# A seven-product feed-forward: matrix sums of the weight blocks made earlier, on VectorE, and kept in device memory

## The chip, the cores and the metric

One core of one Trainium2 chip runs the whole program. The metric is the device time of one execution in microseconds (us). Engines: TensorE (PE; its weight loads are PEld), VectorE (DVE), ScalarE (ACT), GpSimd (POOL), SyncE (SP, which issues the DMAs here).

## The reference

Two layers over 512 tokens of width 1024, in float32. Each layer mixes tokens in three ways (a gated delta net, a sparse attention, a gated recurrence), projects the result back, and then runs a feed-forward block. Only this block matters here:

```python
def conv_geglu_ffn(h, w_up, conv_w, w_down):
    up = causal_depthwise_conv(h @ w_up, conv_w)
    gate, val = jnp.split(up, 2, axis=-1)
    return (jax.nn.gelu(gate, approximate=True) * val) @ w_down
...
    x = x + rmsnorm(conv_geglu_ffn(h, ffn_w_up[l], ffn_conv[l], ffn_w_down[l]), g_ffn_post[l])
```

`w_up` is 1024 x 5632, `w_down` is 2816 x 1024.

## The kernel before

Every float32 product is made of three matmuls on split operands: an operand is rounded to a high part by ACT (line 123, `split`), and the low part is the difference, a subtraction on DVE or on POOL (line 124). The names end in h or hi and l or lo.

**The up stage** (`ffn`, line 927 on) goes over 22 pairs of column tiles (j). For each of the 44 tiles, `project` loads one weight tile of 512 KB (`wraw`, two buffers), splits it (`whi`, `wlo`, two buffers each) and runs 24 matmuls of 512 columns into one of two accumulators `p_mm` (lines 181 to 183). `conv` then reads the accumulator, with one ACT pass (line 198) and two DVE passes (line 200), into `u`. DVE multiplies gate and value (line 944). After every odd j, two pairs are combined into the left operands of one block: `as` and `ad` (high and low), `ax`, and the plain sum tile `ak`. So there are 11 blocks, each with 256 rows of `w_down`.

**The down stage** (`down_seven`, line 961 on) computes the 2 x 2 block product with seven products in place of eight, so it needs sums and differences of the four 128 x 512 quarters of each weight block. The quarters arrive as two 512 KB tiles, x and y (both called `wx`). There are two sweeps over the 11 blocks:

- the first (`first_weights`) splits y, makes two sums on DVE (lines 1008, 1009), splits x, and splits `ak` on POOL (`kl`). Its products 2, 1, 6 and 5 take 24 matmuls of a block (line 983);
- the second (`second_weights`) loads x and y again, makes two differences on DVE (lines 1027, 1029) and one sum on POOL (line 1031), and splits the three results, two on DVE, one on POOL (`dl`, `ql`, `wm`). It takes 18 matmuls of a block.

The raw tiles use the six buffers of the up weights (`wraw`, `whi`, `wlo`) in turn, so three blocks are in flight. The split results use four wide tiles (`wm`, two blocks in flight) or small slots of the pool of 68 (`act`). The last blocks' products are held back (`keep`, `hold`) so that they cover the closing norms.

Each engine runs its instructions in a fixed order, which a scheduler sets when the program is built; the order of the calls in the code and the priorities (`first()`) steer it. SP issues all DMAs one after the other; an issue that waits holds those behind it.

Of the kernel before, what the change touches and what calls it, by code (L numbers as in the profile page):

```python
# [9 lines left out]
F32 = mybir.dt.float32  # L10
# [3 lines left out]
OP = mybir.AluOpType  # L14
# [4 lines left out]
T = 512  # L19
P = 128  # L20
NB = 4
D = 1024
KT = 8
NIN = 30
NFF = 22
# [14 lines left out]
def hybrid_encoder_kernel(ctx: ExitStack, tc: tile.TileContext, x, win, wout, wup, wdn, gall, gates,  # L40
                          dncw, ffcw, vecs, hglb, consts, out):
    nc = tc.nc
    V, S, G, PE, SP = nc.vector, nc.scalar, nc.gpsimd, nc.tensor, nc.sync
# [3 lines left out]
    ring = ctx.enter_context(tc.tile_pool(name="ring", bufs=2))  # L47
    ps = ctx.enter_context(tc.tile_pool(name="ps", bufs=2, space=PSUM))

    def first(n=1):  # L50
        return tc.high_priority(offset=n * FIRST)
# [70 lines left out]
    def split(src, hi, lo, eng=V):  # L122
        S.activation(hi, src, AF.Copy)  # L123
        eng.tensor_tensor(lo, src, hi.bitcast(F32), op=OP.subtract)  # L124
# [71 lines left out]
    def conv(dst, acc, w, taps):  # L196
        with first():
            S.activation(dst, acc, AF.Copy, scale=w[:, taps - 1:taps])  # L198
            for s in range(1, taps):
                V.scalar_tensor_tensor(dst[:, s:], acc[:, :T - s], w[:, taps - 1 - s:taps - s], dst[:, s:],  # L200
                                       op0=OP.mult, op1=OP.add)
# [709 lines left out]
    def slot(pool, name, dt=F32R):  # L911
        return pool.tile([P, T], dt, name=name, tag="act", bufs=ACT_SLOTS)
# [10 lines left out]
    def ffn(l, hid, pool, extra):  # L923
        cw = pool.tile([P, 2 * P], F32, name="fcw", tag="fcw", bufs=1)[:, :6 * NFF].rearrange("p (j s) -> p j s", s=3)
        SP.dma_start(cw, ffcw[l])
        half = lambda z, r: z.rearrange("p (i r c) -> p i r c", r=2, c=P)[:, :, r]
        part = lambda z, r: z[:, 2 * P * r:2 * P * r + 2 * P]
        side = lambda z, r: part(z, r).rearrange("p (i c) -> p i c", c=P)
        left, accs, last = [], [], None
        for j in range(NFF):  # L930
            up = pool.tile([P, 2 * T], F32, name="u", tag="u", bufs=2)
            uv = [up[:, :T], up[:, T:]]
            for i in range(2):
                if not accs:
                    n = 3 if j == 0 else 1
                    accs, last = project(hid, [wup[l, 2 * j + i + m] for m in range(n)], COLS2 if n > 1 else ((0, T),),
                                         extra=extra)
                conv(uv[i], accs.pop(0), cw[:, 2 * j + i], 3)
            gelu = S.activation(uv[0], uv[0], AF.Gelu_apprx_tanh)  # L939
            if j % 2 == 0:  # L940
                same, cross = slot(pool, "ak", F32), slot(pool, "ar", F32)
            for r in range(2):
                to = same if r == j % 2 else cross
                V.tensor_tensor(side(to, r), half(uv[0], r), half(uv[1], r), op=OP.mult)
            if j % 2 == 0:
                continue
            rows, both = [[slot(pool, n) for n in (f"{m}h", f"{m}l")] for m in ("as", "ad")]
            diff = slot(pool, "ax")
            V.tensor_tensor(uv[0], same, cross, op=OP.add)  # L949
            split(uv[0], *rows)  # L950
            V.tensor_tensor(part(uv[1], 0), part(cross, 1), part(same, 0), op=OP.subtract)
            V.tensor_tensor(part(uv[1], 1), part(same, 0), part(same, 1), op=OP.add)
            split(uv[1], *both)
            V.tensor_tensor(part(cross, 0), part(cross, 0), part(same, 1), op=OP.subtract)
            split(part(cross, 0), part(diff, 0), part(diff, 1))
            left.append((rows, both, (part(diff, 0), part(diff, 1)), same))
        explog(gelu)
        return left, last

    def down_seven(pool, left, src, gp, xs, finish, after):  # L960
        n = len(left)
        keep, hold = 4, 8
        loads = [0]
        M = {"2": [do("m2"), po_("m2")], "1": [dn("m1"), dn("m1")], "6": [ds("m6"), ds("m6")], "5": [mm("m5"), mm("m5")]}
        begun = set()

        def raw(j):
            k = loads[0]
            loads[0] += 1
            tags = ("wraw", "wraw") if k < 2 or k % 3 == 1 else ("whi", "wlo")  # L970
            xy = [ring.tile([P, D], F32, name="wx", tag=t, bufs=2) for t in tags]
            for i in (1, 0):
                SP.dma_start(xy[i], src[i, j])
            return xy

        def quarter(z, i):
            return z[:, i * T:(i + 1) * T]
# [12 lines left out]
        def wide():  # L990
            return [base.tile([P, 4, T], F32R, name="wm", tag="ht", bufs=4) for _ in range(2)]

        def first_weights(j):
            x, y = raw(j)
            if j == 0:
                ops = [[ring.tile([P, D], F32R, name=t, tag=t, bufs=2) for t in ("whi", "wlo")] for _ in range(2)]
                ya, za = ops
                yw = [[quarter(t, i) for t in ya] for i in range(2)]
                zw = [[quarter(t, i) for t in za] for i in range(2)]
            else:  # L1000
                w = wide()
                ya = [t[:, 0:2].rearrange("p i t -> p (i t)") for t in w]
                za = [t[:, 2:4].rearrange("p i t -> p (i t)") for t in w]
                yw = [[t[:, i] for t in w] for i in range(2)]
                zw = [[t[:, 2 + i] for t in w] for i in range(2)]
            with first():
                split(y, *ya)
                V.tensor_tensor(quarter(x, 0), quarter(x, 0), quarter(y, 1), op=OP.add)
                V.tensor_tensor(quarter(x, 1), quarter(y, 0), quarter(y, 1), op=OP.add)
                split(x, *za)  # L1010
            same = left[j][3]
            kh, kl = slot(pool, "kh"), slot(pool, "kl")
            split(same, kh, kl, G)
            left[j] = left[j][:3] + ((kh, kl),)
            return yw, zw

        def second_weights(j):
            x, y = raw(j)
            if 2 <= j < n - keep:
                w = wide()  # L1020
                dw = [[t[:, i] for t in w] for i in range(3)]
                if j >= n - hold:
                    dw[2] = [slot(pool, "qh"), slot(pool, "ql")]
            else:
                dw = [[slot(pool, "dh"), slot(pool, "dl")] for _ in range(3)]
            with first():
                V.tensor_tensor(quarter(y, 1), quarter(x, 1), quarter(y, 1), op=OP.subtract)  # L1027
                split(quarter(y, 1), *dw[1])
                V.tensor_tensor(quarter(x, 0), quarter(x, 0), quarter(y, 0), op=OP.subtract)
                split(quarter(x, 0), *dw[0])  # L1030
                G.tensor_tensor(quarter(x, 1), quarter(x, 1), quarter(y, 0), op=OP.add)  # L1031
                split(quarter(x, 1), *dw[2], G)
            return dw

        xv = []
# [16 lines left out]
        for i in range(2):  # L1052
            t = slot(pool, "yt", F32)
# [26 lines left out]
        for j in range(2, n):  # L1080
            dw = second_weights(j)
# [33 lines left out]
    hid = Hidden()  # L1115
    with tc.tile_pool(name="start", bufs=1, reuse_waits="tile") as pool:
        xs = load_x(pool, 1)
# [11 lines left out]
    for l in range(L):  # L1129
        hid = mix_phase(l, hid)  # L1130
        with tc.tile_pool(name="ffn", bufs=1, reuse_waits="tile") as pool:
            extra = lambda: [slot(pool, "fw") for _ in range(2)]
            left, last = ffn(l, hid, pool, extra)
            row = lambda k, i: lambda c: bass.AP(tensor=gall.tensor, offset=gall.offset + (k * 4 + i) * D + c.start,
                                                 ap=[[0, P], [1, T]])
            gp = lambda: Halves(pool, "gp", row(l, 3))
            xs = lambda b: Halves(pool, "xb", lambda c: xd[b][:, c])
            if l + 1 < L:
                gn = []
                hid2 = Hidden()  # L1140

                def finish(b, xb):
                    if not gn:
                        gn.append(Halves(pool, "gn", row(l + 1, 0)))
                    norm_block(pool, hid2, b, xb, gn[0], tag="u")
                    xd[b] = tc.dram_tile([P, D], F32, name="xd")
                    for q in range(2):
                        SP.dma_start(xd[b][:, q * T:(q + 1) * T], xb[:, q * T:(q + 1) * T])
            else:
                def finish(b, xb):  # L1150
                    for q in range(2):
                        SP.dma_start(out[b * P:(b + 1) * P, q * T:(q + 1) * T], xb[:, q * T:(q + 1) * T])
            down_seven(pool, left, wdn[l], gp, xs, finish, last)
        hid = hid2


# [78 lines left out]
```

## Time and profile before

| | us |
|---|---|
| median of 3 runs (lowest, highest) | 1446.74 (1445.73, 1454.11) |
| the profiled execution: its own time | 1458.69 |
| the profiled execution: span from first to last instruction | 1456.8 |

All stretches and durations come from the profiled execution, which is 11.95 us longer than the median; differences worked out in it are taken over to the median as they stand. In the trace, the up stages run from 386 to 609.6 us (layer 0) and from 1098 to 1321.1 us (layer 1), the down stages from 609.6 to 738.7 and from 1321.1 to 1449.4 us. Line L983 is `add`, the products of the down stage; L181 to L183 are those of the up stage. An engine's busy share says little by itself: what counts is which engine the others wait for in a stage.

### The profile page before, as it was taken

What the parts mean: (1) busy time and instruction counts of PE and PEld (TensorE: products, weight loads), DVE (VectorE), ACT (ScalarE), POOL (GpSimd) and SP (SyncE); (2) the same over time, 40 slices, a digit from 0 to 9 for tenths busy, and PEclk for the clock granted to TensorE, in tenths of its full rate; (3) what the DMA queues carried; (4) which work ended last, traced back from release to release, by engine and by line L of the source; (5) the groups of instructions that cost most, each with busy time, mean ns of one, the idle gap of its engine ahead of it and who ended that gap; (6) DMA issues with size and microseconds to landing.
All of it is one profiled execution on the core that took longest, in us unless ns stands there. A gap on an engine that the chain in (4) does not pass through costs nothing.

```text
span 1456.8 us, 20429 instructions
## 1 busy us (share of the span) xinstructions
PE 1370.6 (94%) x7560; PEld 1113.0 (76%) x7560; DVE 1110.1 (76%) x1967; ACT 736.2 (51%) x1395; POOL 223.8 (15%) x160
## 2 busy tenths in 40 slices
PE   6999989999999999989789999899999999999987
PEld 5787767868888888767578877678788888886765
DVE  4599974786767767799875999779666776768988
ACT  4355854555543444453453558565654443444533
POOL 2032210010000000054520322102000000003353
PEclk9999996999999999999999999999999999999998
DMA  4433320025233233386524233201342232235852
GB/s 161 121 94 109 102 57 19 15 73 188 89 101 101 88 102 101 115 293 194 180 100 126 88 109 102 59 17 52 123 147 89 100 100 94 95 102 184 280 193 94
DMA packets 59459, 166.04 MB, mean 114 GB/s; under 512 B 15264, under 2 KB 16224, under 8 KB 59360
## 3 DMA queue, kind: packets, MB, share of 16 engines
q1 hardware_dynamic: 59360, 164.73, 34.6%
q8 instruction: 60, 0.98, 0.3%
q14 instruction: 39, 0.32, 0.1%
HBM read 152.36 MB, written 8.95 MB: 111 GB/s over the span
## 4 chain that ended last, share of the span: by engine, by line
PE 64%; DVE 23%; ACT 5%; issue 4%; DMA 3%; POOL 0%; SPq 0%; DVEq 0%; POOLq 0%; ACTq 0%
PE p_mm L182 14%; PE p_mm L183 14%; PE p_mm L181 14%; PE p_m L983 5%; DVE sc L394 3%; DMA wx<-in_wdn_dram 3%; DVE wm L124 3%; DVE m L393 2%; PE p_dn L225 2%; PE p_dn L226 2%; PE p_dn L220 2%; DVE qkv L200 1%; DVE wx L1027 1%; DVE dl L124 1%; DVE wlo L124 1%
## 5 line engine op out<-in xcount | busy, mean ns | idle before, releaser
L181 PE MATMUL p_mm<-hhi,whi 128*128 128x512 f32 (+1 forms) x1232 | 474.4, 386 | 4.1 <-DVE qkv L200 3.9
L182 PE MATMUL p_mm<-hlo,whi 128*128 128x512 f32 (+1 forms) x1232 | 474.2, 385 | 1.6 <-DVE hlo L177 1.6
L183 PE MATMUL p_mm<-hhi,wlo 128*128 128x512 f32 (+1 forms) x1232 | 474.1, 385 | 0.0
L124 DVE TENSOR_TENSOR wlo<-wraw,whi 128x1024 fp32r<-128x1024 f32 x132 | 163.2, 1236 | 176.1 <-ACT whi L123 173.7
L123 ACT ACTIVATE whi<-wraw 128x1024 fp32r<-128x1024 f32 x156 | 165.1, 1058 | 240.9 <-PE p_mm L182 205.9
L181 PEld LDWEIGHTS p_mm<-hhi,whi 128*128 128x128 f32 x1232 | 234.4, 191 | 48.4 <-ACT qkv L198 4.4
L182 PEld LDWEIGHTS p_mm<-hlo,whi 128*128 128x128 f32 x1232 | 234.8, 191 | 44.6 <-DVE hlo L177 2.8
L183 PEld LDWEIGHTS p_mm<-hhi,wlo 128*128 128x128 f32 x1232 | 235.0, 191 | 42.5 <-issue 0.5
L124 POOL TENSOR_TENSOR kl<-ak,kh 128x512 fp32r<-128x512 f32 x22 | 40.4, 1853 | 651.7 <-ACT kh L123 644.9
L200 DVE SCALAR_TENSOR_TENSOR u<-p_mm,fcw,u 128x511 f32<-128x511 f32 (+1 forms) x172 | 128.2, 745 | 7.8 <-ACT u L198 5.5
L124 POOL TENSOR_TENSOR wlo<-wraw,whi 128x1024 fp32r<-128x1024 f32 x24 | 57.5, 2396 | 260.3 <-PE p_mm L183 93.8
L123 ACT ACTIVATE wm<-wx 128x1024 fp32r<-128x1024 f32 (+1 forms) x62 | 53.9, 900 | 63.9 <-PE p_m L983 27.0
L124 DVE TENSOR_TENSOR wm<-wx,wm 128x1024 fp32r<-128x1024 f32 (+1 forms) x60 | 78.0, 1327 | 9.2 <-ACT wm L123 8.9
L939 ACT ACTIVATE u<-u 128x512 f32<-128x512 f32 x44 | 27.9, 633 | 72.9 <-DVE u L200 72.9
L983 PE MATMUL p_m<-wm,ash 128*128 128x512 f32 x160 | 52.2, 399 | 6.9 <-DVE wm L124 5.2
L198 ACT ACTIVATE u<-p_mm,fcw 128x512 f32<-128x512 f32 x86 | 57.6, 670 | 0.0
L200 DVE SCALAR_TENSOR_TENSOR qkv<-p_mm,cw,qkv 128x511 f32<-128x511 f32 (+2 forms) x72 | 53.0, 739 | 5.1 <-ACT qkv L198 4.8
L123 ACT ACTIVATE ash<-u 128x512 fp32r<-128x512 f32 x22 | 14.0, 634 | 80.4 <-DVE u L949 80.4
L983 PE MATMUL p_m<-wm,adh 128*128 128x512 f32 x160 | 52.1, 402 | 2.2 <-DVE wm L124 1.6
L393 DVE MAX8 m<-sc 128x8 f32<-128x512 f32 (+2 forms) x96 | 52.8, 554 | 1.0
L394 DVE MATCH_REPLACE8 sc<-m,sc 128x512 f32<-128x512 f32 (+2 forms) x96 | 51.9, 541 | 0.0
L1031 POOL TENSOR_TENSOR wx<-wx 128x512 f32<-128x512 f32 x22 | 36.6, 1664 | 52.1 <-DVE wx L1027 52.1
(367 smaller groups left out, 2427.0 us busy)
## 6 DMA issues: line engine op xcount, KB each, us to landing
wraw<-in_wup_dram SPq DMA_DIRECT2D x88, 512.0 KB, 3.4
wx<-in_wdn_dram SPq DMA_DIRECT2D x88, 512.0 KB, 4.6
wraw<-in_win_dram SPq DMA_DIRECT2D x60, 512.0 KB, 3.5
wraw<-in_wout_dram SPq DMA_DIRECT2D x16, 512.0 KB, 3.5
xb<-in_x_dram SPq DMA_DIRECT2D x8, 512.0 KB, 6.3
E<-dr SPq DMA_DIRECT2D x8, 512.0 KB, 3.7
xd<-xb SPq DMA_DIRECT2D x8, 512.0 KB, 2.7
xb<-xd SPq DMA_DIRECT2D x16, 256.0 KB, 5.9
```

The source lines that it names most:

```text
L123: S.activation(hi, src, AF.Copy)
L124: eng.tensor_tensor(lo, src, hi.bitcast(F32), op=OP.subtract)
L181: PE.matmul(out_, ah, bh, start=start, stop=False)
L182: PE.matmul(out_, ah, bl, start=False, stop=False)
L183: return PE.matmul(out_, al, bh, start=False, stop=stop)
L198: S.activation(dst, acc, AF.Copy, scale=w[:, taps - 1:taps])
L200: V.scalar_tensor_tensor(dst[:, s:], acc[:, :T - s], w[:, taps - 1 - s:taps - s], dst[:, s:], op0=OP.mult, op1=OP.add)
L220: first = PE.matmul(acc[b], th[:, bs], piece(hi, i, T), start=k == 0, stop=False)
L393: V.max(m8, bias)
L394: V.match_replace(bias, m8, bias, REPL)
L983: p = PE.matmul(M[m][i], al(a[x]), w[y], start=first_, stop=False, skip_group_check=True)
L1031: G.tensor_tensor(quarter(x, 1), quarter(x, 1), quarter(y, 0), op=OP.add)
```

## The change

The five sums and differences of each block move from the two sweeps of the down stage to the up stage. A new function, `weight_sums`, is called at j = 1, 2, 4, 6, 7, 9, 11, 12, 14, 16 and 17. It loads the four quarters in four DMAs of 256 KB, makes the five results with five DVE operations of 128 x 512, and stores them in five DMAs of 256 KB to a scratch tensor in device memory (`wsz`, `wsx`, `wsq`). The sweeps load the results: y and z (512 KB each) in the first, x (512 KB) and q (256 KB) in the second, and only split them. All splits of the sweeps, `kl` and the third one of the second sweep too, are on DVE; POOL has no part in them. `hold` goes from 8 to 6. ACT's roundings and the number of matmuls stay.

```diff
@@ ffn
-        left, accs, last = [], [], None
+        left, accs, last, sums = [], [], None, []
         for j in range(NFF):
+            if len(sums) < NFF // 2 and j % 5 not in (0, 3):
+                sums.append(weight_sums(pool, wdn[l], len(sums)))
...
+    def weight_sums(pool, src, j):
+        x, y, z = [[slot(pool, f"w{m}", F32) for _ in range(2)] for m in "xyz"]
+        for i, t in ((0, x), (1, y)):
+            for q in range(2):
+                SP.dma_start(t[q], src[i, j, :, q * T:(q + 1) * T])
+        for out_, a, b, op in ((z[0], x[0], y[1], OP.add), (z[1], y[0], y[1], OP.add), (x[0], x[0], y[0], OP.subtract),
+                               (y[0], x[1], y[0], OP.add), (x[1], x[1], y[1], OP.subtract)):
+            V.tensor_tensor(out_, a, b, op=op)
+        dz, dx, dq = [tc.dram_tile([P, c], F32, name=f"ws{m}") for m, c in (("z", D), ("x", D), ("q", T))]
+        for d, t in ((dz, z), (dx, x), (dq, y[:1])):
+            for q, h in enumerate(t):
+                SP.dma_start(d[:, q * T:(q + 1) * T], h)
+        return dz, dx, dq
...
@@ down_seven
-        keep, hold = 4, 8
+        keep, hold = 4, 6
...
@@ first_weights
-            x, y = raw(j)
+            y, z = raw(src[1, j], sums[j][0])
...
             with first():
                 split(y, *ya)
-                V.tensor_tensor(quarter(x, 0), quarter(x, 0), quarter(y, 1), op=OP.add)
-                V.tensor_tensor(quarter(x, 1), quarter(y, 0), quarter(y, 1), op=OP.add)
-                split(x, *za)
+                split(z, *za)
             same = left[j][3]
             kh, kl = slot(pool, "kh"), slot(pool, "kl")
-            split(same, kh, kl, G)
+            split(same, kh, kl)
@@ second_weights
-            x, y = raw(j)
+            x, q = raw(sums[j][1], sums[j][2])
...
             with first():
-                V.tensor_tensor(quarter(y, 1), quarter(x, 1), quarter(y, 1), op=OP.subtract)
-                split(quarter(y, 1), *dw[1])
-                V.tensor_tensor(quarter(x, 0), quarter(x, 0), quarter(y, 0), op=OP.subtract)
+                split(quarter(x, 1), *dw[1])
                 split(quarter(x, 0), *dw[0])
-                G.tensor_tensor(quarter(x, 1), quarter(x, 1), quarter(y, 0), op=OP.add)
-                split(quarter(x, 1), *dw[2], G)
+                split(q, *dw[2])
```

Where the instructions go, first on DVE in the up stage of layer 0, around the pairs j = 6 and 7. `wlo` is the split of an up weight, L200 the convolution, `ar` and `ak` the gated products. Before:

```order
L124 TENSOR_TENSOR wlo<-wraw,whi 128x1024
L200 SCALAR_TENSOR_TENSOR u<-p_mm,fcw,u 128x511
L200 SCALAR_TENSOR_TENSOR u<-p_mm,fcw,u 128x510
L944 TENSOR_TENSOR ar<-u 128x256
L944 TENSOR_TENSOR ak<-u 128x256
L949 TENSOR_TENSOR u<-ak,ar 128x512
L951 TENSOR_TENSOR u<-ar,ak 128x256
L952 TENSOR_TENSOR u<-ak 128x256
L954 TENSOR_TENSOR ar<-ar,ak 128x256
L124 TENSOR_TENSOR asl<-u,ash 128x512
L200 SCALAR_TENSOR_TENSOR u<-p_mm,fcw,u 128x511
L124 TENSOR_TENSOR wlo<-wraw,whi 128x1024
```

And now (lines of the changed file; L969 are the new sums):

```order
L124 TENSOR_TENSOR wlo<-wraw,whi 128x1024
L200 SCALAR_TENSOR_TENSOR u<-p_mm,fcw,u 128x511
L200 SCALAR_TENSOR_TENSOR u<-p_mm,fcw,u 128x510
L946 TENSOR_TENSOR ar<-u 128x256
L946 TENSOR_TENSOR ak<-u 128x256
L951 TENSOR_TENSOR u<-ak,ar 128x512
L953 TENSOR_TENSOR u<-ar,ak 128x256
L969 TENSOR_TENSOR wz<-wx,wy 128x512
L969 TENSOR_TENSOR wz<-wy 128x512
L124 TENSOR_TENSOR wlo<-wraw,whi 128x1024
L200 SCALAR_TENSOR_TENSOR u<-p_mm,fcw,u 128x511
L969 TENSOR_TENSOR wx<-wx,wy 128x512
```

The sums stand ahead of the next `wlo` and between the two passes of a convolution; what they displace (`ar`, `asl`) comes later.

On SP, at the start of the up stage of layer 0, the 40 loads of up weights stood in one row; now each sum's loads and stores stand among them (- before, + now; `wraw` is an up weight, `wx` and `wy` the four quarters, `wsz`, `wsx`, `wsq` the stores):

```order
 L925 DMA fcw<-in_ffcw_dram 128x132
-L130 DMA wraw<-in_wup_dram 128x1024 x40
-L973 DMA wx<-in_wdn_dram 128x1024 x13
+L130 DMA wraw<-in_wup_dram 128x1024 x3
+L966 DMA wx<-in_wdn_dram 128x512 x2
+L966 DMA wy<-in_wdn_dram 128x512 x2
+L130 DMA wraw<-in_wup_dram 128x1024
+L973 DMA wsz<-wz 128x512 x2
+L973 DMA wsx<-wx 128x512
+L973 DMA wsq<-wy 128x512
```

An up weight's load now stands behind four loads or behind three or four stores that wait for DVE. The loads of a sum are issued one up weight ahead of the sums that use them.

On DVE at the start of the second sweep (`yu` combines finished products, `wm` are split results). Before:

```order
L1064 TENSOR_TENSOR yu<-p_m_5373,yt 128x512
L1027 TENSOR_TENSOR wx<-wx 128x512
L1029 TENSOR_TENSOR wx<-wx 128x512
L1027 TENSOR_TENSOR wx<-wx 128x512
L124 TENSOR_TENSOR wm<-wx,wm 128x512 x4
L1029 TENSOR_TENSOR wx<-wx 128x512
```

Now:

```order
L1077 TENSOR_TENSOR yu<-p_m_5626,yt 128x512
L124 TENSOR_TENSOR wm<-wx,wm 128x512 x5
L124 TENSOR_TENSOR ql<-wx,qh 128x512 x2
L124 TENSOR_TENSOR wm<-wx,wm 128x512 x5
L124 TENSOR_TENSOR dl<-wx,dh 128x512 x5
```

Only splits are left there; `ql`, and the `dl` that were POOL's, have joined them.

## Rows read from the trace of the kernel before

**Rows 1.** The page: busy time of each engine, its share of the span, instructions.
```profile
PE 1370.6 (94%) x7560; PEld 1113.0 (76%) x7560; DVE 1110.1 (76%) x1967; ACT 736.2 (51%) x1395; POOL 223.8 (15%) x160
```

**Rows 2.** Busy time by stage: up, down, up, down; the last three columns are clock, DMA, rate.
```profile
386.00:609.60 223.60, 223.60 (x990) 185.23 (x990) 156.36 (x239) 94.58 (x135) 0.00 (x0) 1.00 0.30 97
609.60:738.70 129.10, 114.37 (x471) 88.01 (x469) 116.67 (x126) 60.85 (x102) 56.02 (x34) 0.97 0.65 216
1098.00:1321.10 223.10, 223.10 (x986) 184.76 (x986) 155.91 (x238) 93.90 (x135) 0.00 (x0) 1.00 0.30 96
1321.10:1449.40 128.30, 115.22 (x463) 88.43 (x462) 113.80 (x122) 56.62 (x90) 55.49 (x33) 0.95 0.59 200
```

**Rows 3.** PE in order of time: a tile's first matmul, each down stage's first and last.
```profile
604.16 0.39 PE L181 MATMUL p_mm<-hhi,whi 128*128 128x512 f32 x1
...
609.60 0.39 PE L983 MATMUL p_m<-whi,ash 128*128 128x512 f32 x1
...
738.46 0.39 PE L983 MATMUL p_m<-dh,ax 128*128 128x512 f32 x1
...
1321.14 0.39 PE L983 MATMUL p_m<-whi,ash 128*128 128x512 f32 x1
...
1449.06 0.39 PE L983 MATMUL p_m<-dh,ax 128*128 128x512 f32 x1
```

**Rows 4.** PE's waits in the down stage of layer 0: total us, times, longest.
```profile
PE p_m L983 <- DVE wm L124: 6.7, 4, 2.8
PE p_m L983 <- ACT wm L123: 3.4, 4, 2.4
```

**Rows 5.** Groups of the down stage, layer 0: busy, mean ns; idle before, what ended it.
```profile
L124 DVE TENSOR_TENSOR wm<-wx,wm 128x1024 fp32r<-128x1024 f32 x20 | 28.6, 1447 | 2.1 <-ACT wm L123 2.1
L1027 DVE TENSOR_TENSOR wx<-wx 128x512 f32<-128x512 f32 x11 | 11.9, 1081 | 4.1 <-DMA wx<-in_wdn_dram 2.8 <-POOL wx L1031 1.3
L1031 POOL TENSOR_TENSOR wx<-wx 128x512 f32<-128x512 f32 x11 | 18.3, 1667 | 25.8 <-DVE wx L1027 25.8
L123 ACT ACTIVATE wm<-wx 128x1024 fp32r<-128x1024 f32 x20 | 20.7, 1055 | 21.7 <-DVE wx L1009 10.8 <-PE p_m L983 10.0 <-DMA wx<-in_wdn_dram 0.7
```

**Rows 6.** DVE, then POOL, in order of time in the second sweep.
```profile
709.17 1.78 DVE L1027 TENSOR_TENSOR wx<-wx 128x512 f32<-128x512 f32 x1
710.87 0.68 DVE L1029 TENSOR_TENSOR wx<-wx 128x512 f32<-128x512 f32 x1
...
708.84 1.56 POOL L124 TENSOR_TENSOR dl<-wx,dh 128x512 fp32r<-128x512 f32 x1 [0.74 <-ACT dh L123]
```

**Rows 7.** Stretches of 4 us, columns as in rows 2: full traffic, a slow clock, stores.
```profile
618.00:622.00 4.00, 3.68 (x15) 2.16 (x13) 3.28 (x5) 2.02 (x3) 0.00 (x0) 1.00 0.93 370
698.00:702.00 4.00, 2.89 (x7) 2.34 (x8) 3.88 (x4) 1.67 (x3) 2.06 (x2) 0.54 0.46 147
1438.00:1442.00 4.00, 4.00 (x19) 3.34 (x18) 3.21 (x6) 1.80 (x6) 0.00 (x0) 1.00 0.34 131
```

**Rows 8.** Groups on DVE in the up stage of layer 0.
```profile
L124 DVE TENSOR_TENSOR wlo<-wraw,whi 128x1024 fp32r<-128x1024 f32 x40 | 49.0, 1225 | 62.6 <-ACT whi L123 62.5
L949 DVE TENSOR_TENSOR u<-ak,ar 128x512 f32<-128x512 f32 x10 | 6.9, 692 | 0.3
```

**Rows 9.** One tile's period in the up stage: ACT, then DVE, in order of time.
```profile
598.70 1.06 ACT L123 ACTIVATE whi<-wraw 128x1024 fp32r<-128x1024 f32 x1 [0.76 <-PE p_mm L182]
...
599.79 1.23 DVE L124 TENSOR_TENSOR wlo<-wraw,whi 128x1024 fp32r<-128x1024 f32 x1 [1.64 <-ACT whi L123]
600.93 1.53 DVE L200 SCALAR_TENSOR_TENSOR u<-p_mm,fcw,u 128x511 f32<-128x511 f32 x2
```

**Rows 10.** DMA issues (KB, median us to landing); last, `wx`: minimum, median, maximum.
```profile
wraw<-in_wup_dram SPq DMA_DIRECT2D x88, 512.0 KB, 3.4
xb<-xd SPq DMA_DIRECT2D x16, 256.0 KB, 5.9
...
DMA to landing us min/median/max: 3.3/4.6/7.6
```

More of the change, by code (lines that the diff above doesn't have):

```diff
@@ L957, in ffn, with down_seven @@
         explog(gelu)
-        return left, last
-    def down_seven(pool, left, src, gp, xs, finish, after):
+        return left, last, sums
+    def weight_sums(pool, src, j):
[11 more added lines that the diff above has]
+        return dz, dx, dq
+    def down_seven(pool, left, sums, src, gp, xs, finish, after):
         n = len(left)
-        keep, hold = 4, 8
+        keep, hold = 4, 6
         loads = [0]
@@ L965, in down_seven, with raw @@
         begun = set()
-        def raw(j):
+        def raw(*from_):
             k = loads[0]
@@ L970, in raw @@
             tags = ("wraw", "wraw") if k < 2 or k % 3 == 1 else ("whi", "wlo")
[L971 to L974, printed above, removed]
+            got = []
+            for f, t in zip(from_, tags):
+                r = ring.tile([P, D], F32, name="wx", tag=t, bufs=2)[:, :f.shape[-1]]
+                SP.dma_start(r, f)
+                got.append(r)
+            return got
         def quarter(z, i):
@@ L1132, in hybrid_encoder_kernel @@
             extra = lambda: [slot(pool, "fw") for _ in range(2)]
-            left, last = ffn(l, hid, pool, extra)
+            left, last, sums = ffn(l, hid, pool, extra)
             row = lambda k, i: lambda c: bass.AP(tensor=gall.tensor, offset=gall.offset + (k * 4 + i) * D + c.start,
@@ L1152, in finish @@
                         SP.dma_start(out[b * P:(b + 1) * P, q * T:(q + 1) * T], xb[:, q * T:(q + 1) * T])
-            down_seven(pool, left, wdn[l], gp, xs, finish, last)
+            down_seven(pool, left, sums, wdn[l], gp, xs, finish, last)
         hid = hid2
```

## The prediction

> **What bounds the kernel now.** I read the page's busy times first. PE is busy for 94% of the span [rows 1], but its matmuls overlap in the trace, so that share doesn't say whether it waits. I therefore cut the span into its stages [rows 2] and timed PE against its own pace. In the up stage PE is busy for all of 223.6 us, at full clock. One tile begins at 604.16 us and the next work at 609.60, so 24 matmuls take 5.44 us, 0.2267 us each [rows 3]. This is a stage that only PE bounds: a VectorE operation added there costs nothing as long as it doesn't make PE late.
>
> The down stage is different. From its first product to the end of its last it takes 738.46 + 0.23 - 609.60 = 129.1 us in layer 0 and 1449.06 + 0.23 - 1321.14 = 128.2 us in layer 1 [rows 3]. Its matmuls are 11 blocks x (24 + 18) = 462, at PE's own pace 104.7 us. So 24.4 and 23.5 us, 47.8 together, are lost there. That is the most that any change of the down stage's feeding can win. The waits say on whom: on the split weights `wm` from DVE and from ACT [rows 4]. DVE is busy for 116.67 of 129.1 us there and for 156.36 of 223.6 us in the up stage [rows 2]. The waits in the trace are smaller than the loss, since part of it is a slow clock: between 698 and 702 us, just after PE had stood still, the granted clock was 0.54, about the lower of the two levels (1.2 of 2.4 GHz), and matmuls cost twice as much [rows 7].
>
> Why is DVE so busy there? A block of the first sweep costs it two splits of 128x1024 at 1.447 us and two sums at about 1.08 us, 5.1 us, against 5.44 us of PE [rows 5]. In the second sweep it is two differences and two splits of 128x512, at 1.08 us some 4.3 us, against 18 x 0.2267 = 4.08 us. But these operations are dear only in company. The difference at 709.17 took 1.78 us while POOL ran a subtraction from 708.84 to 710.40; the next, with POOL idle, took 0.68 us [rows 6]. In the up stage, where POOL does nothing [rows 2], the same size takes 0.692 us and the 128x1024 split 1.225 us [rows 8]. POOL itself needs 1.667 us for such a sum, and waits for DVE before most of them [rows 5].
>
> **What the change takes out of the sweeps.** Four DVE operations and one POOL operation for each block go, and POOL's splits (`kl`, and the third split of the second sweep) come to DVE. First sweep, by block: 2 x 1.225 + 0.692 = 3.14 us of DVE, in place of 5.1. Second sweep: 3 x 0.692 = 2.08 us, in place of 4.3 and a POOL chain. Both are far under PE's 5.44 and 4.08 us. ACT keeps its roundings: 2 x 1.055 us and a small one in the first sweep, under 3 us [rows 5]. So DVE and POOL leave the path, and what is late next is PE itself, with three leftovers.
>
> - The head of the first sweep: the first blocks' halves pass through the same few raw buffers, so a load (median 4.6 us [rows 10]) and a rounding (1.055 us [rows 5]), 5.7 us, stand in turn with a block's 5.44 us. Two or three such turns and the first rounding, which waits for the last up tile: 2.5 us.
> - The join of the sweeps, where both last blocks' wide tiles must be free before block 2 can be rounded: one rounding and a split, 1.5 us at most of those that are there now.
> - The tail: with `hold` 6 there are 12 matmuls less, 2.7 us, to cover the closing norms; 1 us.
>
> I take 5 us for each layer to remain. The bounds are 0 and, if half of the present loss has another cause (below), 12 us.
>
> The traffic of the sweeps doesn't grow: 1.05 MB by block in the first, 0.79 MB in the place of 1.05 in the second, which at PE's pace is 193 GB/s in both. At 0.93 busy the DMA engines moved 370 GB/s [rows 7].
>
> **What it adds to the up stage.** 55 DVE operations for each layer at 0.692 us: 38.1 us. DVE goes from 156.4 to 194.5 of 223.6 us, 87%. That fits on average, so the question is the single period. In the trace ACT rounds the next weight at 598.70, DVE splits it at 599.79 and the two convolution passes end at 600.93 + 1.53 = 602.46; the accumulator that they free is needed at 604.16 [rows 3, 9]. The margin is 1.70 us. In the order of the changed kernel the fullest period, from one `wlo` to the end of the next, holds both passes (1.53), two gated products and a half-size difference (1.2 together, by size from the 0.692), one full sum (0.69), two of the new sums (1.38) and the `wlo` (1.23): 6.0 us against 5.44. It runs 0.6 us late, and later periods without a sum give that back. By itself this is free.
>
> Loads come next. A pair with a sum moves 9 x 256 KB and two up weights, 3.41 MB in 10.88 us, 313 GB/s; over the 17 pairs it is 43.8 MB in 185 us, 237 GB/s. Loads reached 370/0.93 = 398 GB/s, and stores of the same 2 KB rows 131/0.34 = 385 GB/s [rows 7]. That fits too, without much air.
>
> By the Trainium skill (Perfetto Trace Analysis, DMA Optimizations), transfers in 2 KB pieces pay an overhead that batching into 4 or 8 KB avoids; the change goes from 4 KB rows to 2 KB rows. The stores' 385 GB/s is no worse than the 4 KB rows' 398, so this trace doesn't bear the rule out at 2 KB for stores. If 2 KB rows ran at half rate, the 25.9 MB of sums in a layer would take 130 us and 17.8 MB of up weights 45 us, 175 of 185 us: the stage would still fit, but the quarters would be late, which is the second rival below.
>
> The delicate point is SP's order and the wait that it adds. Four quarter loads are issued right behind an up weight, when DVE has finished one `wlo`; DVE's first sum stands behind the next `wlo` and a convolution pass, about 5.44 + 0.77 = 6.2 us later. The up weight lands after 3.4 us [rows 10], the quarters 0.67 us apart behind it at 390 GB/s: the last at 6.1 us. So the sum comes just in time. If it is late, DVE stands still, with `wlo` and the convolutions queued behind it, and PE waits once the 1.70 us are used up. The stores wait for sums that stand ahead of the `wlo` that frees the next weight's buffer, so they hold no weight back. I take 2 us of PE for each layer. The bounds are 0 and, if every quarter came as late as the latest `wx` load (7.6 us in place of 3.4 [rows 10], so at 10.3 us), 11 x (10.3 - 6.2 - 1.7) = 26 us.
>
> **Sum.** 47.8 - 2 x 5 - 2 x 2 = 33.8 us less. The profiled execution would go from 1458.7 to 1424.9 us, and the median, to which the difference is taken over, from 1446.7 to 1412.9 us.
>
> **Rivals.** *Half of the loss is structure.* ACT's roundings of `wm` also waited for PE to free the wide tiles (10.0 us in layer 0 [rows 5]): two blocks in flight and no more. If these waits, not DVE, set the pace, half of the 47.8 us stays and 24 - 4 = 20 us are won: 1427 us. Against it: with 3.1 us of DVE and 2.7 us of ACT for a block, a tile freed when a block ends is filled again well within the next block's 5.44 us.
>
> *The quarters come late and hold DVE in the up stage.* Without a cost in the up stage the gain is 37.8 us, and 22 sums share it: 1.7 us of PE for each undoes it. With the margin of 1.7 us that is the case from 3.4 us of lateness on, a landing 9.6 us after the up weight's issue. At 10.3 us the loss is 22 x 2.4 = 53 us, and the time 1446.7 + 53 - 37.8 = 1462 us, slower than before. A PE that stands still would lose clock on top [rows 7]. For it: two loads of 256 KB in the busy down stage took 5.9 us [rows 10], and SP can't pass a waiting issue. Against it: the up stage's queue is at 0.30 now [rows 2], and 385 to 398 GB/s are there.
>
> *It doesn't do what it says, as the sweeps are bound by their loads*: at 193 GB/s wanted and 370 seen, I give this nothing of its own.
>
> **How the numbers follow.** The forecast has 0.68, with its own range of 1401 to 1425 us (remaining loss of 0 to 10 us a layer, up stage 0 to 4). The structural rival has 0.16, around 1427 us. The late quarters have 0.16, half of it near no change, half slower by more than 1%. A measurement of this kernel can tell about 1%, 14.5 us, from no change. Faster by more: 0.68 and three quarters of the structural case, 0.80. Within 1%: 0.12. Slower: 0.08. The range for 8 in 10 goes from 1400 us (all of the loss gone would be 1399) to 1438 us, which takes in the structural rival and the milder lateness.
>
> **What would show it.** Right: in the down stages, PE from first to last product in about 110 us, no wait on DVE over 1 us in the steady part, 128x512 operations at 0.69 us throughout, POOL idle, clock near 1.00; in the up stage DVE near 195 us and PE still without gaps, with DMA near 0.6 to 0.7. Wrong: PE waiting in the up stage for `wlo` or an accumulator, with DVE's wait before L969 put down to the quarter loads; or down stages of 120 us in which ACT waits for PE.

## The result and the profile after

| | before | changed |
|---|---|---|
| median, us (lowest to highest), 4 runs of each | 1448.13 (1445.73 to 1454.11) | 1420.12 (1403.10 to 1437.21) |
| the profiled execution: its own time, us | 1458.69 | 1409.51 |
| the profiled execution: span, us | 1456.8 | 1407.7 |

The medians differ by 28.0 us. The ratio is 0.9705 (95% interval 0.9641 to 0.9770); like all ratios below it leaves out executions more than 1.5% above the fastest of the same kernel, here two of the changed one, so it isn't the quotient of the medians, 0.981. Measured again in e8, the medians were 1441.17 and 1410.08 us, 31.1 us less, and the ratio 0.9743 (0.9679 to 0.9807). The forecast was 33.8 us less.

The page of the changed kernel, to lay beside [rows 1]. POOL lost half of its work; everybody else's busy time hardly moved.

```profile
PE 1348.8 (96%) x7560; PEld 1103.3 (78%) x7560; DVE 1080.1 (77%) x2033; ACT 731.9 (52%) x1395; POOL 112.7 (8%) x94
```

The same four stages as in [rows 2]: up, down, up, down; the last three columns are the granted clock, the DMA share and GB/s.

```profile
362.60:593.70 231.10, 228.29 (x1024) 188.87 (x1023) 190.27 (x295) 97.22 (x139) 0.00 (x0) 1.00 0.62 208
593.70:702.90 109.20, 108.20 (x480) 87.86 (x479) 77.97 (x110) 61.54 (x106) 0.00 (x0) 1.00 0.66 229
1061.50:1293.70 232.20, 228.71 (x1024) 188.97 (x1023) 190.14 (x295) 97.25 (x139) 0.00 (x0) 1.00 0.61 207
1293.70:1399.80 106.10, 105.93 (x463) 85.97 (x461) 72.56 (x102) 54.28 (x90) 0.00 (x0) 1.00 0.60 211
```

In the down stages DVE fell from 116.67 to 77.97 us, POOL to nothing, the stretch from 129.1 to 109.2 us, and the clock is 1.00 throughout. In the up stages DVE stands at 190 us and DMA at 0.62, and PE is no longer busy for all of the stretch: 2.8 us are missing in layer 0, 3.5 in layer 1.

To compare runs I cut every trace at the same events: the up stage from its first convolution pass (line 198) to the first product of the down stage, the down stage from there to the end of its last product. Sums of both layers, in us:

| | up | down | both |
|---|---|---|---|
| before | 455.3 | 257.2 | 712.5 |
| changed | 463.5 | 215.2 | 678.7 |
| difference | +8.2 | -42.0 | -33.8 |
| forecast | +4 | -37.8 | -33.8 |

The kernel before was traced once. Its up stages come out the same to the tenth in e1, e4 and e5; how much its down stages vary isn't known.

The spans differ by 49.1 us, 15.3 more than that. Those lie in the mixing stages, whose code the change doesn't touch: up to the first convolution pass of layer 0 the changed kernel took 19.4 us less, from the last product of layer 0 to that pass of layer 1 3.8 us more. A stretch at half clock comes there in some executions and not in others, so the stage lengths tell more than the times. Here it is, in the columns of [rows 2], first in the trace of before (layer 0), then in that of the changed kernel, which has full clock in the same window of layer 0 and the slow stretch in layer 1. In the windows of 20 us with a clock of 0.50 PE is busy all the time.

```profile
220.00:240.00 20.00, 18.29 (x383) 13.96 (x382) 12.13 (x29) 11.60 (x23) 0.00 (x0) 0.68 0.09 29
240.00:260.00 20.00, 20.00 (x167) 16.55 (x166) 7.03 (x19) 7.88 (x17) 0.00 (x0) 0.50 0.00 1
```

```profile
240.00:260.00 20.00, 18.41 (x152) 16.30 (x151) 17.52 (x43) 13.97 (x26) 2.36 (x1) 1.00 0.03 5
...
920.00:940.00 20.00, 20.00 (x212) 16.38 (x211) 7.42 (x20) 6.00 (x12) 0.00 (x0) 0.50 0.01 2
```

The cut at the last product leaves one thing out. In layer 0 transposes for the next layer stand among the last products: all 16 in the changed kernel, 8 before, none in e5 below. Behind the last product PE goes on at once with the next layer's projection in the changed kernel, and waits for 2.35 us before and for 7.67 us in e5 (in this order):

```profile
702.92 0.28 PE L181 MATMUL p_mm<-hhi,whi 128*128 128x256 f32 x1
```

```profile
741.19 0.63 PE L173 MATMUL p_tp<-cst,hn 128*128 128x128 f32 x4 [2.35 <-DVE hn L170]
```

```profile
721.30 1.94 PE L173 MATMUL p_tp<-cst,hn 128*128 128x128 f32 x8 [7.67 <-DVE hn L170]
```

From the last product of layer 0 to the up stage of layer 1, first e3 (sums in the up stage), then e5 (sums in the sweeps), at nearly the same clock:

```profile
700.41:1047.12 346.71, 330.82 (x2281) 270.24 (x2280) 269.65 (x608) 206.87 (x455) 56.20 (x44) 0.99 0.28 91
```

```profile
712.41:1065.88 353.47, 332.64 (x2297) 271.25 (x2296) 275.19 (x619) 211.12 (x468) 56.03 (x44) 0.99 0.28 91
```

All seven traces with at least some of the sums in the up stage, or without sums, lie between 344.9 us (e7, mean clock 0.995) and 358.8 (e8, 0.952), near a straight line between the two. By that line one expects 348 us at e5's clock of 0.986, 349 at that of before (0.981) and 353 at e1's (0.971). They took 353.5, 354.8 and 358.0. So, by this estimate, the changed kernel wins another 5 us or so between the layers, which the stage sums don't show. `hold` fell from 8 to 6 in all seven, and no run tells its part from that of the sums.

**The down stage.** The groups of DVE in layer 0, which answer to [rows 5], and then the longest waits there. (Total us, times, longest.)

```profile
L124 DVE TENSOR_TENSOR wm<-wx,wm 128x1024 fp32r<-128x1024 f32 x20 | 23.7, 1220 | 12.8 <-ACT wm L123 12.8
L124 DVE TENSOR_TENSOR dl<-wx,dh 128x512 fp32r<-128x512 f32 x18 | 11.3, 684 | 0.8 <-ACT dh L123 0.8
L124 DVE TENSOR_TENSOR kl<-ak,kh 128x512 fp32r<-128x512 f32 x11 | 7.0, 682 | 0.0
...
ACT wm L123 <- PE p_m L1001: 27.1, 10, 5.2
DVE wm L124 <- ACT wm L123: 19.3, 10, 3.2
```

The 128x1024 split went from 1447 to 1220 ns, and the 128x512 splits take 0.68 us. The direction of the waits has turned round. Before, PE waited for `wm` [rows 4]; now ACT waits for PE to free the wide tiles, DVE waits for ACT, and PE waits for them for 0.13 us in all: its only gap over 0.2 us from the first to the last product of layer 0 is this one, at a transpose for the next layer.

```profile
695.36 0.66 PE L173 MATMUL p_tp<-cst,hn 128*128 128x128 f32 x4 [0.85 <-DVE hn L170]
```

**The up stage.** The waits of layer 0 (DVE's first new sum is line 969), and one place in order of time: SP's issues, DVE, then PE.

```profile
DVE wz L969 <- DMA wy<-in_wdn_dram: 9.9, 7, 2.4
PE p_mm L181 <- DVE u L200: 2.8, 3, 1.6
```

```profile
436.35 0.33 SPq L130 DMA_DIRECT2D wraw<-in_wup_dram  x1
437.57 0.32 SPq L973 DMA_DIRECT2D wsx<-wx  x1
437.94 0.94 SPq L966 DMA_DIRECT2D wx<-in_wdn_dram  x2
438.92 0.93 SPq L966 DMA_DIRECT2D wy<-in_wdn_dram  x2
...
443.10 0.42 DVE L953 TENSOR_TENSOR u<-ar,ak 128x256 f32<-128x256 f32 x1
445.56 0.69 DVE L969 TENSOR_TENSOR wz<-wx,wy 128x512 f32<-128x512 f32 x1 [2.04 <-DMA wy<-in_wdn_dram]
...
450.05 0.47 PE L181 MATMUL p_mm<-hhi,whi 128*128 128x512 f32 x1 [1.08 <-DVE u L200]
```

The quarter loads of this sum stand on SP behind a store of the sum before (437.57), which waits for DVE's operation. They go out 1.6 us after the up weight, the last is there at 445.5, 9.1 us after that weight's issue, and DVE, which came to the sum at 443.5, stands still for 2.04 us. What is behind it is late: the pass that frees PE's accumulator (line 200) ends so late that PE stands still for 1.08 us at 450.05. There are three such gaps over 0.1 us in layer 0 and three in layer 1, with 6.2 us in all.

Only four of the 22 sums have a store ahead of their loads; 5.5 of the 6.2 us stand behind those four. It holds the loads up for 1.2 us. But quarters come late without it too. Here is the sum before, again SP and then DVE:

```profile
424.91 0.33 SPq L130 DMA_DIRECT2D wraw<-in_wup_dram  x1
425.29 0.90 SPq L966 DMA_DIRECT2D wx<-in_wdn_dram  x2
426.24 0.91 SPq L966 DMA_DIRECT2D wy<-in_wdn_dram  x2
...
431.66 0.69 DVE L969 TENSOR_TENSOR wz<-wx,wy 128x512 f32<-128x512 f32 x1 [0.88 <-DMA wy<-in_wdn_dram]
```

The loads go out right behind the up weight, DVE comes to the sum 5.9 us after that weight's issue and can begin 6.7 us after it. In the 13 places of this kind where DVE waits it begins 6.7 to 8.5 us after the weight's issue; the waits are 0.19 to 2.05 us, 13.5 in all, and cost PE only 0.7 us.

### The profile page after: what moved, and what is told of

It reads as the page before. It is cut to its first block, busy times and chain, and to the rows that moved or that the text cites. A ratio compares the mean times of both kernels' runs of the same rounds, so it can differ in the third digit from the quotient of the medians.

```text
span 1407.7 us, 20684 instructions
## 1 busy us (share of the span) xinstructions
PE 1348.8 (96%) x7560; PEld 1103.3 (78%) x7560; DVE 1080.1 (77%) x2033; ACT 731.9 (52%) x1395; POOL 112.7 (8%) x94
## 4 chain that ended last, share of the span: by engine, by line
PE 70%; DVE 18%; ACT 5%; DMA 3%; issue 3%; SPq 0%; DVEq 0%; ACTq 0%
PE p_mm L182 14%; PE p_mm L181 14%; PE p_mm L183 14%; PE p_m L1001 11%; DVE sc L394 3%; PE p_dn L225 2%; PE p_dn L226 2%; DVE m L393 2%; PE p_dn L220 2%; DMA wy<-in_wdn_dram 2%; DVE qkv L200 2%; DVE wlo L124 1%; PE p_dsao L422 1%; PE p_hlo L782 1%; PE p_tp L173 1%
## 5 line engine op out<-in xcount | busy, mean ns | idle before, releaser
L182 PEld LDWEIGHTS p_mm<-hlo,whi 128*128 128x128 f32 x1232 | 233.4, 189 | 43.5 <-DVE hlo L177 2.2
L200 DVE SCALAR_TENSOR_TENSOR u<-p_mm,fcw,u 128x511 f32<-128x511 f32 (+1 forms) x172 | 127.9, 744 | 1.8 <-ACT u L198 0.3
L124 DVE TENSOR_TENSOR wm<-wx,wm 128x1024 fp32r<-128x1024 f32 (+1 forms) x66 | 64.0, 1010 | 37.0 <-ACT wm L123 37.0
L200 DVE SCALAR_TENSOR_TENSOR qkv<-p_mm,cw,qkv 128x511 f32<-128x511 f32 (+2 forms) x72 | 53.0, 739 | 5.1 <-ACT qkv L198 4.8
L393 DVE MAX8 m<-sc 128x8 f32<-128x512 f32 (+2 forms) x96 | 52.8, 554 | 1.0
L448 POOL COPY z<-cst 32x512 f32<-32x512 f32 x8 | 5.6, 698 | 422.1 <-DVE hn L170 418.9
L173 PE MATMUL p_tp<-cst,hn 128*128 128x128 f32 x128 | 21.9, 300 | 17.0 <-DVE hn L170 15.4
L1001 PEld LDWEIGHTS p_m<-wm,ash 128*128 128x128 f32 x160 | 29.9, 188 | 8.3 <-DVE wm L124 1.8
```

The lines of the kernel that those rows point to most:

```text
L173: PE.transpose(p[:, k * P:(k + 1) * P], h[:, (4 * q + k) * P:(4 * q + k + 1) * P], ident)
L182: PE.matmul(out_, ah, bl, start=False, stop=False)
L393: V.max(m8, bias)
L1001: p = PE.matmul(M[m][i], al(a[x]), w[y], start=first_, stop=False, skip_group_check=True)
```

## The experiments

All of them stand beside before, 1451.86 us for the first four and 1441.17 for the second four. Stage sums are cut as above.

**e1: POOL's work to DVE, nothing else.** The kernel before, with three edits:

```diff
-            split(same, kh, kl, G)
+            split(same, kh, kl)
...
-                G.tensor_tensor(quarter(x, 1), quarter(x, 1), quarter(y, 0), op=OP.add)
-                split(quarter(x, 1), *dw[2], G)
+                V.tensor_tensor(quarter(x, 1), quarter(x, 1), quarter(y, 0), op=OP.add)
+                split(quarter(x, 1), *dw[2])
```

Expected:

> Kernel before, with POOL's work in the sweeps (the third sum and all its splits) moved to DVE; the sums stay in the sweeps, the up stage is untouched. Lengths from first to last product, both layers together: down stages 257.3 us before, 215.1 us in the changed kernel; up stages (first convolution to first product) 455.4 and 463.5 us. Theory A (the price was DVE's work in the sweeps, and it had to leave them): DVE has 2 x 1.225 + 2 x 0.69 + 0.69 = 4.5 us for a block's 5.44 us in the first sweep and 6 x 0.69 = 4.15 for 4.08 us in the second, so the second stays bound: down stages 235 to 250 us. Rival B (the price was POOL's company, which made a 0.68 us operation 1.78 us; moving the sums was not needed): all 128x512 operations at 0.69 us, down stages 215 to 228 us, up stages 455 us, in the sum as fast as the changed kernel or faster.

Measured: 1420.04 us (1416.76 to 1424.91), ratio 0.9822 (0.9739 to 0.9904). Up 455.3, down 233.4: DVE has more to do than in the kernel before, and yet 23.8 of the 42.0 us are won. The groups of layer 0 say why: the differences that took 1081 ns in company [rows 5] take 686 alone.

```profile
L124 DVE TENSOR_TENSOR wm<-wx,wm 128x1024 fp32r<-128x1024 f32 x20 | 23.8, 1220 | 1.7 <-ACT wm L123 1.5
L1027 DVE TENSOR_TENSOR wx<-wx 128x512 f32<-128x512 f32 x11 | 7.5, 686 | 3.0 <-DMA wx<-in_wdn_dram 3.0
L1031 DVE TENSOR_TENSOR wx<-wx 128x512 f32<-128x512 f32 x11 | 7.5, 683 | 0.0
```

Most of the gaps that are left stand at the join of the sweeps: PE in order of time, and the stretch from there to the end of the stage, in which the mean clock was 0.94 (0.50 from 662.42 to 669.25 us).

```profile
663.63 0.79 PE L983 MATMUL p_m<-dh,kh 128*128 128x512 f32 x1 [3.31 <-ACT yt L1055]
...
666.33 0.80 PE L983 MATMUL p_m<-dh,kh 128*128 128x512 f32 x1 [1.05 <-DVE yt L1056]
...
656.20:713.30 57.10, 52.70 (x225) 42.07 (x223) 52.41 (x88) 28.71 (x60) 0.00 (x0) 0.94 0.62 214
```

DVE is busy for 52.4 of 57.1 us in this part, so the sums do fill it up: 233.4 lies between the two theories.

**e2: the changed kernel, with POOL's two splits back on POOL.**

```diff
-            split(same, kh, kl)
+            split(same, kh, kl, G)
...
-                split(q, *dw[2])
+                split(q, *dw[2], G)
```

Expected:

> Changed kernel, with kl and the third split of the second sweep given back to POOL; the sums stay in the up stage. Theory A (amount of work): DVE has less to do than in the changed kernel, down stages stay at 215 us or fall. Rival B (company): DVE's splits of 128x512 and 128x1024 beside POOL's are stretched to 1.7 us and more and PE waits again: down stages 222 to 240 us, against 215.1. Up stages 463 us by both.

Measured: 1421.16 us (one run). Up 463.3, down 219.9, 4.7 us more than the changed kernel. The company makes itself felt at once, in layer 0 on both engines:

```profile
L124 DVE TENSOR_TENSOR wm<-wx,wm 128x1024 fp32r<-128x1024 f32 x20 | 28.4, 1454 | 13.3 <-ACT wm L123 13.3
L124 POOL TENSOR_TENSOR kl<-ak,kh 128x512 fp32r<-128x512 f32 x11 | 22.2, 2042 | 318.8 <-DMA wx<-wsz 313.2 <-ACT kh L123 5.5
L124 DVE TENSOR_TENSOR dl<-wx,dh 128x512 fp32r<-128x512 f32 x12 | 10.7, 930 | 2.0 <-ACT dh L123 2.0
...
PE p_tp L173 <- DVE hn L170: 1.9, 1, 1.9
PE p_m L1001 <- DVE dl L124: 0.2, 1, 0.2
PE p_m L1001 <- DVE wm L124: 0.2, 1, 0.2
```

PE's products wait 0.4 us for it. The measured 219.9 lies between the two theories. Layer 1 takes 106.7 us, after 106.1 in the changed kernel. The other 4.1 us are in layer 0: the gap at a transpose is 1.9 us in place of 0.85, and the clock fell to 0.50 for a while behind it. That POOL is the reason isn't shown, since this gap was 1.3 to 1.7 us in e4, e7 and e8 too, where POOL is idle. With the sums gone DVE has room, and the company costs little: the two parts of the change cover the same loss, and their gains don't add.

**e3: the loads of the quarters one sum earlier.** The changed kernel, with `weight_sums` cut in two; the loads for the next sum are issued before the operations of this one.

```diff
-                sums.append(weight_sums(pool, wdn[l], len(sums)))
+                if ready is None:
+                    ready = weight_quarters(pool, wdn[l], 0)
+                quarters, ready = ready, None
+                if len(sums) + 1 < NFF // 2:
+                    ready = weight_quarters(pool, wdn[l], len(sums) + 1)
+                sums.append(weight_sums(pool, quarters))
```

Expected:

> Changed kernel, with each sum's four quarter loads issued one sum earlier; everything else as there. The changed kernel's up stages are 8.1 us longer than before's, and DVE waits 22.6 us in front of the first sum for the last quarter. Theory C (late quarters hold DVE): that wait falls under 5 us and the up stages go to 455 to 458 us, down stages stay at 215 us. Rival D (DVE is too full, or the queue's traffic delays the up weights): up stages stay at 461 us or more although the wait in front of the sums is gone.

Measured: 1404.38 us (1391.03 to 1417.94), ratio 0.9642 (0.9536 to 0.9748). Up 456.5, down 215.4. No DVE operation of the up stage waits for a quarter any more, and PE has two gaps left in layer 0, of 0.20 and 0.10 us. 7.0 of the 8.2 us of the up stage were the late quarters. The edit moves the loads ahead of everything that can make them late, so it doesn't tell the store ahead of them from a slow landing.

**e4: no sums at all in the up stage.** The sweeps read weight quarters in their place, so this kernel leaves the sums out.

```diff
-                sums.append(weight_sums(pool, wdn[l], len(sums)))
+                sums.append((wdn[l][0, len(sums)], wdn[l][0, len(sums)], wdn[l][1, len(sums)][:, :T]))
```

Expected:

> Changed kernel without the sums: the up stage has neither their loads, operations nor stores, and the sweeps load quarters of the weights in the place of the sums, so that the result leaves out the sums. By all theories the up stages are 455 to 456 us as before; this run gives what the sweeps are worth by themselves: down stages 215 us if the sums' traffic in the up stage leaves nothing behind, less if the first loads of the sweep came late because of it.

Measured: 1396.93 us (one run). Up 455.3, the length before to the tenth, down 217.9, 2.7 us more than the changed kernel. So the whole 8.2 us come from the new work of the up stage, and the down stage isn't shorter where it reads inputs in place of results just stored.

**e5: sums in the sweeps, the join's order mended.** The kernel of e1, in which the second early block is worked on after the drain of the first sweep's accumulators:

```diff
-        early = [(j, second_weights(j)) for j in range(2)]
+        early = [(0, second_weights(0))]
+        loaded = raw(1)
...
             us.append(u)
+        early.append((1, second_weights(1, loaded)))
```

Expected:

> The run without POOL with one more edit: the second early block's sums and splits are called after the accumulators of the first sweep are drained, so that ACT's two copies and VectorE's six additions at the join stand ahead of them; the loads stay where they were. The sums stay in the sweeps, nothing goes to device memory. Theory A (with POOL gone VectorE keeps pace, and what was left of the run without POOL, 18 us over two layers, is the join's order and the slower clock behind its gap): the gap of 3.3 us at the join goes, the two down stages take 216 to 224 us together instead of 233.4, the up stages 455.3, so the two stages come to 672 to 680 us, level with or below the changed kernel's 678.7. Theory B (VectorE's sums in the sweeps cost time of their own): the down stages stay at 230 us or more.

Measured: 1418.16 us (1406.03 to 1434.93), ratio 0.9808 (0.9746 to 0.9870). Up 455.3, down 226.2: 7.2 us less than e1, under the 230 of theory B but above the 216 to 224 of theory A. The gap at the join went from 3.31 to 2.18 us and the second one is gone; what is left are smaller ones, of 0.4 to 1.0 us in the second sweep, where PE waits for DVE's `dl`. DVE was busy for 52.8 of the 57.4 us there:

```profile
655.00:712.40 57.40, 54.29 (x228) 42.83 (x227) 52.77 (x88) 27.82 (x56) 0.00 (x0) 0.97 0.65 222
```

Neither theory holds alone. Of the 18.2 us between e1 and the changed kernel the order took 7.2. The other 11.0 us, and the 5 us or so between the layers, go with what still differs: the sums in the sweeps, `hold` at 8, and a join that is better but not closed. e6 takes up the sums.

**e6: only the second sweep's three results in device memory.** The kernel of e3, with the first sweep's two sums back in the sweep:

```diff
-            y, z = raw(src[1, j], sums[j][0])
+            y, x = raw(src[1, j], src[0, j])
...
-                split(z, *za)
+                V.tensor_tensor(quarter(x, 0), quarter(x, 0), quarter(y, 1), op=OP.add)
+                V.tensor_tensor(quarter(x, 1), quarter(y, 0), quarter(y, 1), op=OP.add)
+                split(x, *za)
```

Expected:

> The run with early loads, with only the second sweep's three results made in the up stage and kept in device memory; the first sweep's two sums are made by VectorE in the sweep from the raw halves. If only the second sweep lacks room on VectorE (three sums and three splits of 0.68 us are 4.1 us of its 18 x 0.2267 = 4.08 us per block, against 4.5 of 5.44 us in the first): the down stages take 215 to 218 us as with all five sums moved, and the up stages at most 456.5. If the first sweep lacks it too: waits of PE for VectorE's splits in the first sweep, the down stages at 222 us or more.

Measured: 1411.28 us (1406.03 to 1416.40), ratio 0.9788 (0.9738 to 0.9839). Up 457.1, down 222.8, so the first sweep lacks room too, but in one place alone, its second block. In both layers this is PE's only gap over 0.4 us among the products:

```profile
608.46 0.68 DVE L1034 TENSOR_TENSOR wx<-wx 128x512 f32<-128x512 f32 x1
609.07 0.68 DVE L1035 TENSOR_TENSOR wx<-wx 128x512 f32<-128x512 f32 x1
...
609.78 2.01 ACT L123 ACTIVATE wm<-wx 128x1024 fp32r<-128x1024 f32 x2 [1.22 <-DVE wx L1035]
...
610.89 0.50 PE L1009 MATMUL p_m<-wm,adh 128*128 128x512 f32 x1 [2.38 <-ACT wm L123]
```

Before 608.46, DVE is still busy with the left operands of the up stage's last block, and the second block's sums stand behind them. The gap accounts for 4.8 of the 7.4 us between e6 and e3. The rest is 0.7 us of gaps just before it, 1.3 us more at the transposes of layer 0, and a lower clock behind the gap of layer 1.

**e7 and e8: e3 and the changed kernel, once more, side by side.**

> The kernel with the loads of the quarters one sum earlier, again, beside the changed kernel on the same chip: the up stages 7 us shorter together (456 to 457 us against 463), the down stages equal within 1 us; the time 0.5% below the changed kernel's, which may be covered by what the mixing stage adds from run to run.

> The changed kernel again. If its stages repeat, the up stages are 463 to 464 us together and the down stages 214.5 to 216; the time differs from other runs only by what the mixing stages do.

Measured: e7 1393.40 us (1391.81 to 1405.50, 6 runs), ratio 0.9687 (0.9641 to 0.9734); e8 1410.08 us (1395.90 to 1423.41, 6 runs), ratio 0.9743 (0.9679 to 0.9807). Stages: e7 up 456.1, down 216.1; e8 up 462.3, down 216.2. The stages repeat within 1.2 us, a little more than e8's expectation allowed. The kernel with early loads is shorter by 6.2 us where it was meant to be, and beats both kernels; its time is 1.2% under that of the changed one, but the two intervals overlap, since the mixing stages differ by more than the edit is worth.

## Why the prediction was right, and where its steps missed

**The pace of PE was the right measure.** 462 matmuls at 0.2267 us, 104.7 us, were to be what remains when nothing is late. The down stage of layer 1 now takes 106.1 us.

**"These operations are dear only in company" holds, and was worth more than the prediction said.** It counted the sums and POOL's leaving as one. e1 and e2 separate them: POOL's leaving alone gives 23.8 us, the sums' leaving with two splits still on POOL 37.3 us (257.2 - 219.9), both together 42.0. In [rows 6] the difference at 709.17 ended at 710.95, 0.55 us after POOL's subtraction, which had begun before it. That is so throughout the two down stages of before: of DVE's operations with both inputs in SBUF that began while POOL ran one, all 46 of 128x512 ended 0.55 or 0.56 us after POOL's, and all 11 of 128x1024 1.08 us after it. The nine 128x512 operations that read an accumulator in place of a second SBUF tile took their 0.67 to 0.69 us. POOL, then two of these nine, in the trace of before:

```profile
677.57 1.74 POOL L124 TENSOR_TENSOR ql<-wx,qh 128x512 fp32r<-128x512 f32 x1
...
678.08 1.28 DVE L1056 TENSOR_TENSOR yt<-p_m,yt 128x512 f32<-128x512 f32 x2
```

By the Trainium skill (SBUF — State Buffer, Summary: rules for kernel authors) that is to be expected: of a VectorE operation with two inputs in SBUF and a GpSimd operation that reads SBUF, the one that issues second blocks until the first is finished. The counts and e1's 0.68 us agree with it, but that 0.55 us behind POOL is less than the 0.68 us of a whole operation.

**"I take 5 us for each layer to remain"** was too much: 215.2 - 209.4 = 5.8 us for both layers in place of 10. The three leftovers that it names, head, join and tail, hardly exist: 0.13 us of gap at the head in layer 0, nothing at the join, 0.85 us near the end. 2.5 us of the 5.8 aren't a loss at all, but 16 transposes for the next layer that stand between layer 0's products. Eight of them stood there before; the prediction took their time for lost. The tail, 1 us a layer, came out the other way in layer 0, by the estimate of 5 us above; behind the last product of layer 1 the end is 0.4 us longer. The 16 transposes:

```profile
L173 PE MATMUL p_tp<-cst,hn 128*128 128x128 f32 x16 | 2.5, 278 | 0.9 <-DVE hn L170 0.8
```

**"So the sum comes just in time"** failed, and with it "2 us of PE for each layer". It had the last quarter at 6.1 us after the up weight's issue and DVE at the sum after 6.2 us. Over both layers DVE waited 17 times, 22.6 us in all. The term that was too small is the landing: behind an up weight with nothing between, DVE could begin 6.7 to 8.5 us after the weight's issue where it waited. The page of the changed kernel has 5.1 us from issue to landing for the second pair of quarters, and the fourth load is issued 1.8 us after the weight: 6.9 us, an estimate from this page and the rows above.

```profile
wy<-in_wdn_dram SPq DMA_DIRECT2D x44, 256.0 KB, 5.1
```

The margin of 1.7 us hid most of that. What reached PE came mostly (5.5 of 6.2 us) from four places, the pairs j = 7 and 17 of each layer, which follow a pair with a sum. In the one shown above the figures were 9.1 us for the quarters and 7.2 us for DVE: there the loads stand on SP behind a store that waits for DVE. The prediction looked at the stores only for whether they hold an up weight back, and didn't ask what they do to the next quarters. The up stages cost 8.2 us in place of 4; with the loads issued a sum earlier, 1.2.

**The sum was right because these two misses are equal**: 4.2 us less remained than taken, and 4.2 us more were paid. Each lies inside the bounds given, but that they cancel, and that the forecast's 33.8 us is the 33.8 us of the stages, is luck. The medians moved by 28.0 and 31.1 us. They hold two things that the stages don't: the 5 us or so between the layers, and the clock of the mixing stages, which took 709.5 us (e3) to 736.7 us (before) in the traces, both layers together. How the difference divides between them isn't shown.

**The rivals.** *Half of the loss is structure*: it fell. ACT's waits for PE at the wide tiles were 13.6 us in layer 0 (10.0 of them for the 128x1024 ones [rows 5]) and are 27.1 us now, while the stage got shorter by 20 us. This is the wait of an engine with time to spare. *The quarters come late and hold DVE*: the mechanism is there as described, L969 waiting for the quarter loads included, but the longest wait was 2.4 us, and its deciding point was 3.4 us of lateness. *Bound by loads*: nothing of it at 211 to 229 GB/s. The wait of before that is not in [rows 5]:

```profile
ACT wm L123 <- PE p_m L983: 13.6, 6, 3.6
```

**What it said would be seen**: down stages of about 110 us (109.2 and 106.1), 128x512 operations at 0.69 us (0.68), POOL idle, clock 1.00, DVE near 195 us in the up stage (190), DMA 0.6 to 0.7 (0.62): all there. "PE still without gaps" in the up stage was wrong, by six gaps.

By the Trainium skill (Perfetto Trace Analysis, DMA Optimizations) transfers under 2 KB pay an overhead, and batching 2 KB into 4 or 8 KB can raise the throughput much; the prediction put the overhead at 2 KB itself. The changed up stage moves 208 GB/s with the DMA engines 0.62 busy, which is 335 GB/s for a full one; the up stage of before, all in 4 KB rows, moved 97 at 0.30, 323 GB/s [rows 2]. This trace shows no such overhead at 2 KB. e3 moves the same rows and its up stages cost 1.2 us: what cost time was when the loads are issued.

## What to carry to other kernels

When two engines slow each other down, try first what happens if one of them stops: here DVE, the busiest engine of the stage, took over POOL's work and the two down stages got 24 us shorter together. A load that is only just in time is late sooner or later: add up its issues too (0.47 us each here), list what stands ahead of it in the issuing queue, above all a store that waits for an engine, and issue it a step earlier where there is room. And when a forecast agrees with the time, check its terms by stage; two misses may have met. Check also what happens just outside the cut.

## What the runs showed of the hardware

- DVE's additions and subtractions of two operands in SBUF take 0.68 us for 128x512 and 1.22 us for 128x1024 with POOL idle. With POOL at work beside them for part of the time the means were 0.93 and 1.45 us (e2).
- The two engines hold each other up in both directions. In the down stages of before, POOL's operations that began while DVE ran one with two SBUF inputs ended 1.12 to 1.21 us after it, all 65. POOL's splits of 128x512 took 1.29 us with DVE idle beside them (680.54 and 683.67 us in e2), and 2.04 us in the mean for `kl` there.
- Gaps of 1.1 to 1.6 us of PE in the up stage left the granted clock at 1.00. Longer ones did not always: the clock fell to 0.50 at e1's gaps of 3.31 and 1.05 us, at 2.18 us in e5 and 2.46 us in e6 (layer 1), and stayed at 1.00 at 2.38 us in e6 (layer 0).
- The granted clock can be 0.50, the lower of the two levels, for 20 us on end in which PE is busy throughout and DMA all but idle, in one execution, and 1.00 in the same window of another kernel's with the same mixing code.
- Rows of 2 KB moved as fast for a busy DMA engine as rows of 4 KB: 335 GB/s in the mixed traffic of the changed up stage, 323 GB/s with 4 KB rows alone.
